# The convolution's part of the output projection for six of nine row tiles, computed among the attention heads

## The chip, the cores and the metric

The program runs on one core of a Trainium2 chip. The metric is device microseconds (us) of one execution. Three executions of the kernel before took 1584.36, 1586.79 and 1588.87 us, a median of 1586.79 us.

The engines are TensorE (PE, with its weight loads as PEld), VectorE (DVE), ScalarE (ACT), GpSimd (POOL) and SyncE (SP), which here issues the DMAs. Each works through its own instructions strictly in the order in which they are laid down.

## The reference

One layer of a streaming encoder: 1024 prompt rows, 8 samples of 16 rows (nine tiles of 128 rows in all) and D = 1024. One input projection feeds two branches. The first is differential attention: the prompt's rows look at the prompt, each sample at its cache of 1024 keys. The second is a gated causal convolution, a LayerNorm and a swish. One output projection joins both.

```python
z = h @ w_in
...
o = (rmsnorm(o, g_sub) * (1.0 - lam_init)).reshape(B, T, ATTN_WIDTH)
a, gate = jnp.split(zu, 2, axis=-1)
c = a * jax.nn.sigmoid(gate)
...
cv = jax.nn.silu(layernorm(depthwise_causal_conv(c_hist, w_conv, b_conv), ln_g, ln_b))
x = x + jnp.concatenate([o, cv], axis=-1) @ w_out
x = x + cross_attend(rmsnorm(x, g_cross), mk, mv, w_mq, g_mq, w_mo)
```

`o` and `cv` are 512 columns each, so `@ w_out` is the sum of two products with 512 rows of `w_out` each; the lower half, `cv @ w_out[512:]`, is what is moved here. The memory's keys and values (`mem @ w_mk`, `mem @ w_mv`) and an MLP complete the layer.

## The kernel before

All is float32. A product is computed as three matmuls on split operands (`mm3`, lines 123 to 125: high by high, high by low, low by high). A 128x512 block of the output projection from four blocks of 128 rows of `w_out` thus takes 12 matmuls of 512 columns.

The stages are: input projection and convolution taps (to about 297 us), attention (297 to 585 us), output projection (540 to 667 us), cross-attention, MLP. The taps leave the convolution's sums in DRAM (`dacc`).

The attention is written as generators that `weave` (L920) merges by position: each has a start and an end between 0 and 1 (`WP`, `WS`, `WL`, `WM`), and the one that is furthest behind is asked next. A scheduler then orders the instructions of each engine, with the offsets `PRI` as priorities. The generators:

- `prompt_stream` (L719): 4 heads of 8 tiles. A tile's scores go to a PSUM bank `sc` (2 banks), DVE adds the bias and finds the minimum (L679), ACT takes the exponential (L681), DVE joins the two maps (L688), PE transposes the weights (`pT`, bank `tr`, L699) and multiplies by the values (`po`, L704); the result goes to DRAM (`mix`).
- `sample_stream` (L834): per sample four loads of keys (`kr`, 512 KB, pool `wsk` of 4 buffers), transposes (`kT`), scores (`ss`), transposes of the weights (`wt`), four loads of values (`vu`), products (`spo`).
- `conv_norm` (L573): for each group of three tiles a load (`al`), transposes (`cvt`, bank `tr`), statistics and normalization on DVE (L584, L592), transposes back (`cvT`, L598), tanh and scale on ACT (L602, L604), two POOL operations (L605, L606), one store to DRAM (`dcv`, L607). It does so for four column tiles per group, with one buffer each of `sl` and `zt`.
- `memory_stream` (L856): two loads of memory tokens into buffers of the keys' pool, then the products `mk` and `mv` in the banks `sc`, with weights loaded as they come (`wmk`, `wmv`). Its operand is the tile `mem`, the only one of its pool.

After them `mixed_conv` (L1003) reads `dcv` back and splits it (L1008, L1009), and `proj_add` (L1047) multiplies: `n` is the half of the output columns, and tile `pj` the bank. The residual `x` is read from the input into `xr` (`load_xr`, L1043) and added by DVE (L1051). Then `mixed_attention` (L1011) reads `mix` back, transposes it (`omT`) and splits it, and `proj_add` multiplies by the upper half of `w_out`. The matmuls that read tile `MT` are the convolution's part, those that read `HC` the attention's.

Of the kernel before, what the change touches and what calls it, by code (L numbers as in the profile page):

```python
# [10 lines left out]
F32 = mybir.dt.float32  # L11
# [7 lines left out]
P = 128  # L19
# [34 lines left out]
TRS = ("tr", "sc", "tr", "sc", "kT", "sx")  # L54
WP, WS, WL, WM = (0, 1), (0, 1), (.2, .8), (.2, .8)
AB = {"rq": 2, "kS": 2, "rv": 4, "qs": 2, "p": (3, 1), "wT": 2}
# [3 lines left out]
def f32(ap):  # L60
    return ap.bitcast(F32)
# [3 lines left out]
def kernel(  # L65
# [53 lines left out]
    def load_w_plain(src, n, name, ring=None):  # L119
        return load_w([(lambda u: u[:, :n], src)], n, name, ring)  # L120
# [445 lines left out]
    dm = dram.tile([8, 8, 16, P], F32, name="dm")  # L566
    dcv = dram.tile([3, P, 4, 384], F32, name="dcv")
    PB = dict(PB1)
# [3 lines left out]

    def conv_norm():  # L573

        for g in range(3):
            xn = []
# [18 lines left out]
            for ct in range(4):  # L595
                ps = bk("tr", f"cvT{g}_{ct}")
                for j in range(3):
                    pe.transpose(ps[:, j * P:(j + 1) * P], xn[j][:, ct * P:(ct + 1) * P], ident)  # L598
                sg = wl.tile([P, 384], F32, name=f"sl{g}_{ct}", tag="sl", bufs=1)

                hg, hb = hln[:, ct:ct + 1], hln[:, 4 + ct:5 + ct]
                act.activation(sg, ps[:, :384], AF.Tanh, scale=hg, bias=hb)  # L602
                zt = wl.tile([P, 384], F32, name=f"zt{g}_{ct}", tag="zt", bufs=1)
                act.activation(zt, ps[:, :384], AF.Identity, scale=hg, bias=hb)  # L604
                pool.tensor_mul(sg, sg, zt)  # L605
                pool.tensor_add(zt, zt, sg)  # L606
                sp.dma_start(dcv[g, :, ct], zt)  # L607
                yield
# [243 lines left out]
    def mhalf(name):  # L852
        return rpool.tile([P, 512], F32, name=name, tag="r")


    def memory_stream():  # L856
        vm = []
        mh = wlm.tile([P, 2, 2, 4, 256], R32, name="mem", bufs=1)
        for t in range(2):
# [60 lines left out]
    def weave(*streams):  # L920

        live = [[it, n, a, z, 0, p] for it, n, a, z, p in streams]
        while live:
# [14 lines left out]
    wk = p2.enter_context(tc.tile_pool(name="wkA", bufs=2, reuse_waits="tile"))  # L938
    weave((prompt_stream(), 200, *WP, PRI[0]), (conv_norm(), 21, *WL, PRI[1]), (samples, 132, *WS, PRI[2]),
          (memory_stream(), 26, *WM, PRI[3]))  # L940
    p2.close()
# [61 lines left out]
    def mixed_conv(g):  # L1003
        mT[g][1] = new_group("m", g, 1)
        for c in range(4):
            zc = rpool.tile([P, 512], F32, name=f"zc{g}_{c}", tag="r")[:, :384]
            sp.dma_start(zc, dcv[g, :, c])
            act.copy(mT[g][1][:, 0, c, :], zc)  # L1008
            (pool if c % 2 else dve).tensor_sub(mT[g][1][:, 1, c, :], zc, f32(mT[g][1][:, 0, c, :]))  # L1009
# [33 lines left out]
    def load_xr(t):  # L1043
        for n in range(2):
            sp.dma_start(xr[t][n], xf[t][:, n * 512:(n + 1) * 512])

# [21 lines left out]

    def load_wo(k0, n):
        return [load_w_plain(w_out[0, (k0 + k) * P:(k0 + k + 1) * P, n * 512:(n + 1) * 512], 512, f"wo{n}_{k0 + k}")  # L1070
                for k in range(4)]

    for n in range(2):
        wo = load_wo(4, n)
        for g in range(3):
            if n == 0:
                mixed_conv(g)
            for t in range(3 * g, 3 * g + 3):
                if n == 0:
                    load_xr(t)  # L1080
                proj_add(mT, wo, t, n, 4)
    wo = load_wo(0, 0)
    for g in range(3):
        mixed_attention(g)
        for t in range(3 * g, 3 * g + 3):
            proj_add(mT, wo, t, 0)
    wo = load_wo(0, 1)
    memory_operands()
# [573 lines left out]
```

## Time and profile before

| | |
|---|---|
| three runs, median | 1586.79 us |
| profiled execution | 1584.48 us |
| its span, first to last instruction | 1582.7 us |
| mean granted clock of TensorE, share of full speed | 0.986 |
| PE busy | 1503.6 us, 95% |
| PEld busy | 1297.8 us, 82% |
| DVE busy | 1098.6 us, 69% |
| ACT busy | 733.0 us, 46% |
| POOL busy | 295.9 us, 19% |

The span is 1.8 us shorter than the execution. PE counts as busy from the start of a matmul to its modelled end; consecutive matmuls overlap, so a busy PE can still be waiting for operands between starts. Idle time in a view is that of an engine between its instructions, with what ended it.

### The profile page before, as it was taken

What the parts mean: (1) busy time and instruction counts of PE and PEld (TensorE: products, weight loads), DVE (VectorE), ACT (ScalarE), POOL (GpSimd) and SP (SyncE); (2) the same over time, 40 slices, a digit from 0 to 9 for tenths busy, and PEclk for the clock granted to TensorE, in tenths of its full rate; (3) what the DMA queues carried; (4) which work ended last, traced back from release to release, by engine and by line L of the source; (5) the groups of instructions that cost most, each with busy time, mean ns of one, the idle gap of its engine ahead of it and who ended that gap; (6) DMA issues with size and microseconds to landing.
All of it is one profiled execution on the core that took longest, in us unless ns stands there. A gap on an engine that the chain in (4) does not pass through costs nothing.

```text
span 1582.7 us, 25633 instructions
## 1 busy us (share of the span) xinstructions
PE 1503.6 (95%) x9326; PEld 1297.8 (82%) x9326; DVE 1098.6 (69%) x1984; ACT 733.0 (46%) x1530; POOL 295.9 (19%) x410
## 2 busy tenths in 40 slices
PE   7999989879899899999999899999999999999998
PEld 7989787667678688886679899999998887788887
DVE  5999999975756754535758776667565457995564
ACT  6312011486778642635656444444354443354442
POOL 5344682032544330231010000000000000000000
PEclk9999999999999999999999899999999999899999
DMA  6423242567776553103422654444384465653442
GB/s 196 145 82 100 84 136 98 187 210 233 234 243 213 194 168 106 51 24 114 145 85 88 191 179 132 160 156 151 125 259 156 142 206 184 218 172 94 124 135 93
DMA packets 187122, 237.88 MB, mean 150 GB/s; under 512 B 23851, under 2 KB 101717, under 8 KB 186996
## 3 DMA queue, kind: packets, MB, share of 16 engines
q1 hardware_dynamic: 186996, 236.25, 46.5%
q8 instruction: 73, 1.20, 0.3%
q14 instruction: 53, 0.43, 0.1%
HBM read 172.59 MB, written 63.60 MB: 149 GB/s over the span
## 4 chain that ended last, share of the span: by engine, by line
PE 67%; DVE 7%; ACT 5%; DMA 4%; issue 2%; POOL 1%; SPq 1%; DVEq 0%; ACTq 0%; POOLq 0%
PE p L123 13%; PE p L124 13%; PE p L125 13%; PE pj L123 3%; PE pj L125 3%; PE pj L124 3%; DVE acc L307 1%; PE po L704 1%; PE kT L768 1%; PE q L123 1%; PE q L124 1%; PE q L125 1%; PE z L124 1%; PE z L125 1%; PE z L123 1%
## 5 line engine op out<-in xcount | busy, mean ns | idle before, releaser
L124 PE MATMUL p<-Bp,Ap 128*128 128x512 f32 x448 | 176.6, 394 | 0.3 <-DVE Bp L1532 0.2
L125 PE MATMUL p<-Bp,Ap 128*128 128x512 f32 x448 | 176.1, 393 | 0.0
L307 DVE SCALAR_TENSOR_TENSOR acc<-cp,wc,acc 128x1024 f32<-128x1024 f32 (+2 forms) x150 | 167.5, 1119 | 1.2
L123 PE MATMUL p<-Bp,Ap 128*128 128x512 f32 x448 | 159.9, 393 | 7.0 <-ACT Bp L1531 6.0
L1531 ACT CAST Ap<-w_xb 128x512 fp32r<-128x512 f32 x112 | 69.5, 621 | 175.2 <-PE p L125 128.8
L1532 DVE TENSOR_TENSOR Ap<-w_xb,Ap 128x512 fp32r<-128x512 f32 x112 | 77.3, 690 | 102.7 <-ACT Ap L1531 102.6
L123 PE MATMUL p<-b_t,s 128*128 128x288 f32 x384 | 114.9, 299 | 6.2 <-ACT s L1284 6.2
L124 PE MATMUL p<-b_t,s 128*128 128x288 f32 x384 | 114.9, 299 | 0.0
L125 PE MATMUL p<-b_t,s 128*128 128x288 f32 x384 | 114.5, 299 | 0.0
L123 PEld LDWEIGHTS p<-Bp,Ap 128*128 128x128 f32 x448 | 84.2, 189 | 26.0 <-ACT Bp L1531 7.4
L124 PEld LDWEIGHTS p<-Bp,Ap 128*128 128x128 f32 x448 | 85.2, 190 | 19.4 <-DVE Bp L1532 1.4
L125 PEld LDWEIGHTS p<-Bp,Ap 128*128 128x128 f32 x448 | 85.2, 190 | 17.7
L124 PE MATMUL z<-wqkv,h 128*128 128x512 f32 x216 | 85.6, 396 | 1.7 <-DVE wqkv L116 1.6
L123 PE MATMUL z<-wqkv,h 128*128 128x512 f32 x216 | 86.2, 399 | 0.0
L125 PE MATMUL z<-wqkv,h 128*128 128x512 f32 x216 | 85.3, 395 | 0.0
L1368 ACT ACTIVATE o<-o 128x576 f32<-128x576 f32 x64 | 43.9, 686 | 79.9 <-DVE o L1378 32.3
L123 PEld LDWEIGHTS p<-b_t,s 128*128 128x128 f32 x384 | 73.4, 191 | 6.4 <-ACT s L1284 6.4
L123 PE MATMUL p<-b_b,a 128*128 128x288 f32 x256 | 75.8, 296 | 0.0
L124 PE MATMUL p<-b_b,a 128*128 128x288 f32 x256 | 75.7, 296 | 0.0
L125 PE MATMUL p<-b_b,a 128*128 128x288 f32 x256 | 75.6, 296 | 0.0
L124 PEld LDWEIGHTS p<-b_t,s 128*128 128x128 f32 x384 | 73.5, 191 | 0.0
L1051 DVE TENSOR_TENSOR XP<-pj,XP 128x512 f32<-128x512 f32 x54 | 37.1, 689 | 52.3 <-PE pj L125 52.1
(513 smaller groups left out, 4319.7 us busy)
## 6 DMA issues: line engine op xcount, KB each, us to landing
kr<-in_cache_k_dram SPq DMA_DIRECT2D x32, 512.0 KB
vu<-in_cache_v_dram SPq DMA_DIRECT2D x32, 512.0 KB
w1t<-in_w_ff_dram SPq DMA_DIRECT2D x32, 512.0 KB
w_xb<-ds SPq DMA_DIRECT2D x64, 256.0 KB
da<-o SPq DMA_DIRECT2D x48, 256.0 KB
w_xb<-da SPq DMA_DIRECT2D x48, 256.0 KB
ds<-o SPq DMA_DIRECT2D x32, 256.0 KB
dxr<-XP SPq DMA_DIRECT2D x18, 256.0 KB
```

The source lines that it names most:

```text
L123: pe.matmul(out, lh, rh, start=first, stop=False)
L124: pe.matmul(out, lh, rl, start=False, stop=False)
L125: pe.matmul(out, ll, rh, start=False, stop=last)
L307: dve.scalar_tensor_tensor(out=out, in0=cp[:, lo + j:hi + j], scalar=wj, in1=out, op0=ALU.mult, op1=ALU.add)
L704: pe.matmul(po, wT[:, j * P:(j + 1) * P], vss[h][jb][:, j], start=4 * jb + j == 0, stop=4 * jb + j == i)
L768: pe.transpose(ps[:, h * 256 + t * P:h * 256 + (t + 1) * P], kr[:, t, (2 * hp + h) * P:(2 * hp + h + 1) * P], ident)
L1051: dve.tensor_add(xr[t][n], ps, xr[t][n])
L1368: act.activation(c, c, AF.Relu)
L1531: act.copy(u[:, 0], src)
L1532: dve.tensor_sub(u[:, 1], src, f32(u[:, 0]))
```

## The change

Tiles 0 to 5 of the convolution's projection move into the attention. A new generator `conv_stream` is chained behind `memory_stream` as one stream of 68 steps: it loads the eight blocks of the lower half of `w_out`, runs `conv_norm` for groups 0 and 1, keeps the result in SBUF (`mc`, split at once, instead of by way of `dcv`), and for each of 6 tiles and 2 halves loads a half row block of `x` (`xc`), multiplies in a bank `sc` (tile `pc`), adds, and stores the sum to DRAM (`dxc`). Both `mc` and the memory's operand use the one buffer of tag `mem`. `load_xr` later reads `dxc` in place of the input. Group 2 (tiles 6 to 8) keeps the old way. `WL` becomes (.02, .3) and `WM` (.02, 1).

```diff
-WP, WS, WL, WM = (0, 1), (0, 1), (.2, .8), (.2, .8)
+WP, WS, WL, WM = (0, 1), (0, 1), (.02, .3), (.02, 1)
...
-    dcv = dram.tile([3, P, 4, 384], F32, name="dcv")
+    dcv = dram.tile([P, 4, 384], F32, name="dcv")
+    dxc = [dram.tile([P, D], F32, name=f"dxc{t}") for t in range(6)]
+    wo = [[], []]
...
-    def conv_norm():
-        for g in range(3):
+    def conv_norm(g, out):
+        if True:
...
-                sp.dma_start(dcv[g, :, ct], zt)
+                out(ct, zt)
                 yield
...
+    def conv_stream():
+        for n in range(2):
+            for k in range(4):
+                wo[n].append(load_wo(4, n, k))
+                if k % 2:
+                    yield
+        for g in range(2):
+            mc = wlm.tile([P, 4096], R32, name=f"mc{g}", tag="mem")[:, :3072].rearrange("p (h k c) -> p h k c", h=2, k=4)
+            def take(ct, zt):
+                act.copy(mc[:, 0, ct], zt)
+                dve.tensor_sub(mc[:, 1, ct], zt, f32(mc[:, 0, ct]))
+            yield from conv_norm(g, take)
+            for j in range(3):
+                t, c = 3 * g + j, slice(j * P, (j + 1) * P)
+                for n in range(2):
+                    xt = rpool.tile([P, 512], F32, name=f"xc{t}_{n}", tag="r")
+                    sp.dma_start(xt, xf[t][:, n * 512:(n + 1) * 512])
+                    ps = bk("sc", f"pc{t}_{n}")
+                    for k in range(4):
+                        mm3(ps, mc[:, 0, k, c], mc[:, 1, k, c], wo[n][k][:, 0], wo[n][k][:, 1], k == 0, k == 3)
+                        if k == 1:
+                            yield
+                    dve.tensor_add(xt, ps, xt)
+                    sp.dma_start(dxc[t][:, n * 512:(n + 1) * 512], xt)
+                    yield
...
-        mh = wlm.tile([P, 2, 2, 4, 256], R32, name="mem", bufs=1)
+        mh = wlm.tile([P, 4096], R32, name="mem", tag="mem").rearrange("p (a b c d) -> p a b c d", a=2, b=2, c=4)
...
-    weave((prompt_stream(), 200, *WP, PRI[0]), (conv_norm(), 21, *WL, PRI[1]), (samples, 132, *WS, PRI[2]),
-          (memory_stream(), 26, *WM, PRI[3]))
+    weave((prompt_stream(), 200, *WP, PRI[0]), (samples, 132, *WS, PRI[2]),
+          (conv_norm(2, lambda ct, zt: sp.dma_start(dcv[:, ct], zt)), 7, *WL, PRI[1]),
+          (chain(memory_stream(), conv_stream()), 68, *WM, PRI[3]))
...
-            sp.dma_start(xr[t][n], xf[t][:, n * 512:(n + 1) * 512])
+            sp.dma_start(xr[t][n], (xf[t] if t > 5 else dxc[t])[:, n * 512:(n + 1) * 512])
...
+    mixed_conv(2)
+    for t in (6, 7, 8, 0, 1, 2, 3, 4, 5):
+        load_xr(t)
     for n in range(2):
-        wo = load_wo(4, n)
...
+        for t in range(6, 9):
+            proj_add(mT, wo[n], t, n, 4)
```

Three places in PE's order show what moves. The first is at the first samples. Before, PE transposes the memory tokens (`memT`) beside the weights of the second sample (`wt1`), when it is at the prompt's tile 7 of head 0 (`sc0_7`); `kT2_` are the keys of the third sample:

```order
L674 MATMUL sc0_7_1_0_3451<-kS0_0_2759,qs0_1_3005 128x512
L675 MATMUL sc0_7_1_0_3451<-kS0_0_2759,ql1_2750 128x512
L768 MATMUL kT2_0_0_0_3557<-ident_69,kr2_0_3554 128x128 x2
L865 MATMUL memT0_0_3372<-ident_69,mem0_3370 128x128
L794 MATMUL ss1_2_3407<-k8_917,zq_915 32x128 x4
L865 MATMUL memT0_0_3372<-ident_69,mem0_3370 128x128 x3
```

After, they stand beside the weights of the first sample (`wt0`) and the keys of the second (`kr1_`), when the prompt is at tile 3 (`sc0_3` a few rows earlier) and its first product (`po0_0`) still stands behind them:

```order
L900 MATMUL memT0_1_2862<-ident_69,mem0_2847 128x128 x4
L771 MATMUL kT1_0_1_1_3400<-ident_69,kr1_1_3368 128x128 x4
L813 MATMUL wt0_8_3199<-ident_69,sp0_2733 128x128
L780 MATMUL ss1_0_3260<-ku1_0_1_3370,zq_915 32x256 x4
L771 MATMUL kT1_1_0_0_3445<-ident_69,kr1_2_3442 128x128 x4
L828 MATMUL spo0_3330<-vu0_0_3331,wt0_3123 32x128 x8
L828 MATMUL spo0_3330<-vu0_2_3430,wt0_3123 32x128 x8
L702 MATMUL pT0_0_0_2891<-ident_69,p0_0_0_2794 128x128
L771 MATMUL kT1_1_0_1_3480<-ident_69,kr1_2_3442 128x128 x4
L900 MATMUL memT1_0_2910<-ident_69,mem1_2908 128x128 x4
L707 MATMUL po0_0_2890<-vr0_0_2758,wT0_0_0_2893 128x128
```

The memory's work moved ahead by one sample, and the prompt's behind it.

The second place is the start of the second group's products, on PE, in the prompt's last head (`3_`): `pc3_0` and `pc3_1` are the two halves of tile 3, `wo0_5` is block 5 of the first half, `cvT1_3` the last column tile of the branch.

```order
L601 MATMUL cvT1_3_6057<-ident_69,xn5_5841 128x128
L123 MATMUL pc3_1_6195<-wo1_4_4538,mc1_5697 128x512
L124 MATMUL pc3_1_6195<-wo1_4_4538,mc1_5697 128x512
L125 MATMUL pc3_1_6195<-wo1_4_4538,mc1_5697 128x512
L123 MATMUL pc3_0_6112<-wo0_5_4449,mc1_5697 128x512
L124 MATMUL pc3_0_6112<-wo0_5_4449,mc1_5697 128x512
L123 MATMUL pc3_1_6195<-wo1_5_4543,mc1_5697 128x512
L124 MATMUL pc3_1_6195<-wo1_5_4543,mc1_5697 128x512
L125 MATMUL pc3_0_6112<-wo0_5_4449,mc1_5697 128x512
L125 MATMUL pc3_1_6195<-wo1_5_4543,mc1_5697 128x512
L707 MATMUL po3_0_6036<-vr3_0_5725,wT3_0_0_6039 128x128
```

The two halves run side by side, block by block; the next scores, `sc3_3_1`, stand behind the last block of both. Before, nothing like it stands there: the last head ran beside matmuls `pj` of tiles whose operands were complete, as here, with the prompt's tiles 4 to 6:

```order
L124 MATMUL pj3_0_6667<-wo0_5_6570,MT0_6552 128x512
L704 MATMUL po3_4_6223<-vr3_0_5568,wT3_4_0_6229 128x128 x4
L704 MATMUL po3_4_6223<-vr3_1_6037,wT3_4_1_6283 128x128
L674 MATMUL sc3_6_0_1_6323<-kS3_1_6044,qs3_1_6079 128x384
L675 MATMUL sc3_6_0_1_6323<-kS3_1_6044,ql1_2750 128x384
L674 MATMUL sc3_6_1_0_6347<-kS3_0_5575,qs3_1_6079 128x512
L675 MATMUL sc3_6_1_0_6347<-kS3_0_5575,ql1_2750 128x512
L125 MATMUL pj3_0_6667<-wo0_5_6570,MT1_6553 128x512
```

The scores moved behind the blocks of the branch. The third place is the end of the attention, on PE. Before, 26 matmuls `pj` stand between the last product `po3_7` and the first transpose `omT` of the attention's output, and 60 more among the transposes. After, two:

```order
L123 MATMUL pj8_1_6929<-wo1_7_4602,MT0_6812 128x512
L707 MATMUL po3_7_6754<-vr3_0_5725,wT3_7_0_6760 128x128 x4
L707 MATMUL po3_7_6754<-vr3_1_6221,wT3_7_1_6771 128x128 x4
L124 MATMUL pj8_1_6929<-wo1_7_4602,MT0_6812 128x512
L125 MATMUL pj8_1_6929<-wo1_7_4602,MT1_6813 128x512
L1073 MATMUL omT0_0_6969<-ident_69,om0_6963 128x128
```

The matmuls that stood behind the attention moved ahead of its end.

## Rows read from the trace of the kernel before

**Rows 1.** The page, part 1: span; busy us, share of the span, instructions of each engine.
```profile
span 1582.7 us, 25633 instructions
...
PE 1503.6 (95%) x9326; PEld 1297.8 (82%) x9326; DVE 1098.6 (69%) x1984; ACT 733.0 (46%) x1530; POOL 295.9 (19%) x410
```

**Rows 2.** Stretches of the attention: length, busy us (instructions) by engine, clock, DMA, GB/s.
```profile
297.00:380.00 83.00, 64.94 (x603) 47.81 (x603) 59.89 (x155) 62.40 (x150) 18.70 (x40) 0.94 0.70 230
380.00:500.00 120.00, 111.19 (x1130) 90.48 (x1132) 82.27 (x222) 93.37 (x218) 58.80 (x95) 1.00 0.75 235
500.00:540.00 40.00, 34.66 (x354) 28.57 (x353) 24.42 (x61) 31.14 (x77) 16.14 (x25) 0.91 0.52 169
540.00:608.00 68.00, 68.00 (x357) 57.14 (x358) 40.57 (x81) 26.91 (x62) 18.59 (x26) 1.00 0.55 181
```

**Rows 3.** The same view, the attention before the projection joins, as one stretch.
```profile
297.00:540.00 243.00, 210.79 (x2079) 166.85 (x2079) 166.58 (x436) 186.91 (x443) 93.64 (x159) 0.96 0.70 222
```

**Rows 4.** Timeline of PE: start us, us, instruction; two matmuls of the projection, twelve apart.
```profile
605.78 0.40 PE L124 MATMUL pj<-wo,MT 128*128 128x512 f32 x1
...
608.58 0.39 PE L124 MATMUL pj<-wo,HC 128*128 128x512 f32 x1
```

**Rows 5.** Chain of waits, all the program: start us, us, what; three loads on it.
```profile
340.33 4.31 DMA wmk_1r<-in_w_mk_dram
...
477.52 8.00 DMA wmv_3r<-in_w_mv_dram
...
533.46 4.69 DMA vu<-in_cache_v_dram
```

**Rows 6.** Chain of waits, 297 to 400 us; its short pieces of PE work.
```profile
338.98 0.23 PE sc L674
...
363.11 0.89 PE po L704 x8
364.00 0.45 PE kT L768 x4
```

**Rows 7.** The same view as rows 2, the stretch of the memory weights.
```profile
357.00:362.00 5.00, 4.96 (x48) 3.02 (x48) 2.01 (x5) 1.87 (x6) 1.95 (x2) 0.50 0.02 7
```

**Rows 8.** Tile view of the memory tokens, their loads: ns min/median/max, first and last start.
```profile
L861 SPq DMA_DIRECT2D mem<-in_mem_prompt_dram x2: 345/346/346, 319.1 to 326.7; - x2
```

**Rows 9.** Groups on DVE by form, 297 to 586 us: busy us, mean ns, idle before.
```profile
L641 DVE SCALAR_TENSOR_TENSOR ql<-qst,gqk,qs 64x512 fp32r<-64x512 f32 x16 | 12.0, 749 | 14.6 <-ACT qs L640 14.6
L629 DVE TENSOR_TENSOR kS<-kst,kS 64x512 fp32r<-64x512 f32 x16 | 11.0, 689 | 17.2 <-ACT kS L628 16.8
L679 DVE CUSTOM_DVE_ANT_0 p<-sc,biasm 128x512 f32<-128x512 f32 x16 | 11.0, 689 | 7.4 <-PE sc L675 6.9
...
L592 DVE TENSOR_SCALAR xn<-cvt,bmv,vrs 128x512 f32<-128x512 f32 x9 | 7.3, 806 | 1.0 <-POOL vrs L139 0.9
L584 DVE BATCH_NORM_STATS2 bst<-cvt 128x6 f32<-128x512 f32 x9 | 6.3, 695 | 0.5 <-PE cvt L582 0.4
...
L688 DVE SCALAR_TENSOR_TENSOR p<-p,cc,p 128x1024 f32<-128x1024 f32 x4 | 5.6, 1407 | 0.1
```

**Rows 10.** Tile views of the convolution branch: sl and zt, then zc.
```profile
L602 ACT ACTIVATE sl<-cvT,hln x12: 654/671/677, 388.1 to 516.8; 128x384 f32<-128x384 f32 x12
...
L605 POOL TENSOR_TENSOR sl<-sl,zt x12: 993/1008/1022, 389.4 to 518.5; 128x384 f32<-128x384 f32 x12
L606 POOL TENSOR_TENSOR zt<-zt,sl x12: 992/1004/1859, 390.5 to 519.6; 128x384 f32<-128x384 f32 x12
...
L1008 ACT CAST MT<-zc x12: 499/513/518, 539.4 to 560.3; 128x384 fp32r<-128x384 f32 x12
L1009 DVE TENSOR_TENSOR MT<-zc,MT x6: 554/686/1105, 540.4 to 559.9; 128x384 fp32r<-128x384 f32 x6
```

**Rows 11.** Tile views of the projection and of the attention products: first and last start.
```profile
L123 PE MATMUL pj<-wo,HC x72: 390/394/484, 608.3 to 666.1; 128*128 128x512 f32 x72
...
L704 PE MATMUL po<-vr,wT x288: 270/275/422, 314.8 to 584.7; 128*128 128x128 f32 x144
```

More of the change, by code (lines that the diff above doesn't have):

```diff
@@ L853, in mhalf, with load_wo @@
         return rpool.tile([P, 512], F32, name=name, tag="r")
+    def load_wo(k0, n, k):
+        return load_w_plain(w_out[0, (k0 + k) * P:(k0 + k + 1) * P, n * 512:(n + 1) * 512], 512, f"wo{n}_{k0 + k}")
+    def conv_stream():
[23 more added lines that the diff above has]
+                    yield
     def memory_stream():
         vm = []
-        mh = wlm.tile([P, 2, 2, 4, 256], R32, name="mem", bufs=1)
+        mh = wlm.tile([P, 4096], R32, name="mem", tag="mem").rearrange("p (a b c d) -> p a b c d", a=2, b=2, c=4)
         for t in range(2):
@@ L1006, in mixed_conv @@
             zc = rpool.tile([P, 512], F32, name=f"zc{g}_{c}", tag="r")[:, :384]
-            sp.dma_start(zc, dcv[g, :, c])
+            sp.dma_start(zc, dcv[:, c])
             act.copy(mT[g][1][:, 0, c, :], zc)
@@ L1067, in square_sum @@
         return ms2
-    def load_wo(k0, n):
-        return [load_w_plain(w_out[0, (k0 + k) * P:(k0 + k + 1) * P, n * 512:(n + 1) * 512], 512, f"wo{n}_{k0 + k}")
-                for k in range(4)]
+    mixed_conv(2)
+    for t in (6, 7, 8, 0, 1, 2, 3, 4, 5):
+        load_xr(t)
     for n in range(2):
-        wo = load_wo(4, n)
[L1075 to L1082, printed above, removed]
+        for t in range(6, 9):
+            proj_add(mT, wo[n], t, n, 4)
+    wo = [load_wo(0, 0, k) for k in range(4)]
     for g in range(3):
@@ L1086 @@
             proj_add(mT, wo, t, 0)
-    wo = load_wo(0, 1)
+    wo = [load_wo(0, 1, k) for k in range(4)]
     memory_operands()
```

## The prediction

> **What bounds the kernel now.** I read the page's first part, then the attention by stretches, then the chain of waits, then the groups and tiles of the steps that move. PE is busy 95% of the span, more than any other engine [rows 1]. The change takes no matmul away: it moves 6 tiles x 2 halves x 12 = 144 matmuls of 512 columns. Two of the projection start 2.80 us apart with twelve between them, so one costs 0.233 us [rows 4] and the 144 cost 33.5 us, before and after. Its whole effect is thus on PE's waits.
>
> Where are they? In 297 to 540 us PE is busy 210.8 of 243 us: 32.2 us idle, 18.1 of them in the first 83 us, 8.8 in the next 120, 5.3 in the next 40 [rows 2, 3]. From 540 to 608 us, where the conv products now stand among the last head, it is never idle and the clock is full [rows 2]. So the products are already a filler: they hide the waits of the last head, and the change takes 144 of 216 away from there and puts them where idle time is left. The question is whether they fill it, and what they uncover.
>
> The upper bound of a gain is the 32.2 us. A busy share counts overlapped matmuls as busy, so the weight loads are a second reading: they fill 57.1 of the 68 us of the packed stretch, 0.840, and 166.9 of the 243 us, 0.687 [rows 2, 3]. At the packed rate the 243 us hold 166.9 / 0.840 = 198.6 us of work, which leaves 44.4 us of waits. The Trainium skill (Perfetto Trace Analysis, Identifying the Most-Contended Engine) also holds that matmul busy time is a bad measure and that the weight loads' share is the better one; by it the room is 44 us instead of 32. The two shares here differ in that sense; which one the chip pays back no row shows, so it is one of the rivals below.
>
> **The change, part by part.**
>
> *Early, 297 to about 375 us.* WM starts at .02 instead of .2. The memory tokens, loaded at 319 and 327 us before [rows 8], go into two of the four `kr` buffers of the first two samples instead of a later one. The keys' third and fourth loads of the second sample must then wait until the tokens are transposed, and a 512 KB load follows with about 4.7 us in the like of it on the chain [rows 5]; the order leaves about 1 us of PE work as cover for each. By the second sample's weights the order has done 16 instead of 48 `sc` matmuls, 6 instead of 21 `pT`, 3 instead of 21 `po` and 12 more transposes. With 0.23 us for `sc`, 0.45 for four transposes and 0.89 for eight `po` [rows 6] that is 7.4 + 1.7 + 2.0 - 1.3 = 10 us of prompt work less to hide behind. By the third sample 48 earlier `mk` matmuls of 256 columns (half of 0.233 each, 5.6 us) and the prompt's catching up make most of it good. What can go away is a stall on `wmk` (4.31 us on the chain [rows 5]) and its sequel: from 357 to 362 us PE ran at 0.50 of its clock (the lower level, 1.2 GHz) for 5 us, 2.5 us lost, after it had stood with little to do [rows 7]. Two loads uncovered, 7 us, less that stall, 4 to 5 us: I take +2. Bounds: -13 (most of the 18.1 us idle filled) to +10 (all lost cover uncovered).
>
> *Middle, 380 to 540 us.* The 72 products of group 0 (16.8 us) stand among samples whose PE idles 8.8 + 5.3 = 14.1 us [rows 2]. Their operands are complete when they begin. Part of this idle is a wait for a load that comes whatever PE does: `wmv` 8.0 us, `vu` 4.7 us on the chain [rows 5]. I take half, -7. Bounds: -14 to 0.
>
> *The late hole, at the third head's end.* `mc` has one buffer, so group 1's branch may write its operand only when the 72 products of group 0 are through; the order puts its `cvt` transposes right behind `pc2_1`, where the last head also begins. From there to the first column tile DVE stands in order before four reductions (0.689), three statistics (0.695), three normalizations (0.806), two pairs for the next head (0.689 and 0.749) and a joining of the two maps (1.407) [rows 9]: 2.8 + 2.1 + 2.4 + 2.9 + 1.4 = 11.6 us, with the short operations between about 18 us (an estimate: half of it again). PE has about 11 us of work there by the rows of the order (scores, transposes and products at the times above). Then `pc3_0` and `pc3_1` take both `sc` banks, and each of their blocks waits for a column tile: tanh and scale on ACT (0.671 and, of the same form, again 0.671), two on POOL (1.008, 1.004), the copy (0.513) and the difference on DVE (0.554 to 0.686), 4.5 us [rows 10], one after the other, since `sl` and `zt` have one buffer. Three behind the first are 13.5 us, against about 10 us of PE work: 24 products at 0.233, 5.6 us, and transposes, `po` and scores for 4.5 more. The next scores, `sc3_3_1`, stand behind the last block, so ACT and DVE get nothing new from the prompt and it is not caught up. Holes of 7 + 3.5: I take +10. Bounds: +3 (only the column tiles) to +16 (no cover in either, and a lower clock behind them).
>
> *Banks and transfers.* Twelve times `pc` takes one of the two `sc` banks of the prompt or of `mk`/`mv`, and its addition on DVE must free it. Twelve loads `xc` and twelve stores `dxc` of 256 KB are 6.3 MB, less eight stores `dcv` of 197 KB: 4.7 MB more over about 200 us, 23 GB/s on 222 [rows 3], a DMA share of 0.77 instead of 0.70. There is room, but the samples' loads get later. `xc` is hidden by 12 products (2.8 us) only in part. No row shows a `pc`; nearest are the `sc` groups, whose DVE idle before is 7.4 us over 16 [rows 9], 0.46 each. I take +1. Bounds: 0 to 12 x 0.46 = +6.
>
> *The end of the attention.* Before, 86 `pj` stand around and behind the last `po` (584.7 us) before the attention's own start at 608.3 [rows 11]; they hide `mix` on its way through DRAM, the transposes and the split. After, two of the conv products are left and the 72 attention products of tiles 0 to 5 (16.8 us), whose operands were stored long before, cover the last group. The first transposes have less ahead of them. I take +1. Bounds: 0 to +9 (the 608.3 - 584.7 = 23.6 us less 14.6 of other work). The additions `xr` and the splits saved on POOL and DVE stand beside a busy PE and are worth nothing.
>
> Sum: 2 - 7 + 10 + 1 + 1 = +7 us. Against the profiled execution's 1584.5 us (the span of 1582.7 and 1.8 around it) that is 1591.5; the median of the three runs is 2.3 us above it, so I predict 1593.8, rounded 1594.
>
> **The rivals.** *Faster.* The products and the earlier memory work fill idle PE, and the hole stays short, because scores of the last head that stand ahead of the first block feed DVE. Place: 297 to 540 us. Price: early -6 (a third of the 18.1 us), middle -10, hole +4, the rest 0: -12, 1575 us. For it: 32 us idle, and an operand that is ready. Against: the order has both `sc` banks taken while column tiles are made. It decides when the hole is below some 6 us.
>
> *Much faster.* If the waits are the 44.4 us that the weight loads show and half are filled in all stretches, -22: 1565 us. Against it, the longest waits end on loads. The reading of the weight loads as the measure is the skill's page named above.
>
> *No change.* Filled idle and the new hole cancel: -7 to -9 against +7 to +9, 1587 us. This needs only that the early term is -3 instead of +2 and the hole 8.
>
> *Not done as said.* In the order all 144 products stand ahead of the last `po`; this rival is out.
>
> **How the numbers follow.** What a measurement of this kernel can't tell from no change is 0.3%, 4.8 us. The forecast, slower, has 0.44, with its own range +2 to +18; some of it lies inside the 4.8 us, as some of the other cases does, and I let these cancel. No change 0.24, faster 0.26, much faster 0.06; both faster cases are 0.32. The range: below 1573 lies the much faster case and a little of the faster, about 0.1; above 1607 (+20, hole and early term both at their upper ends) another 0.1.
>
> **What would show it.** In the trace after: PE idle and a wait for ACT or DVE at the products of tile 3 (hole of 10 us; under 6 the rival is right); PE idle in the stretch of the second sample's keys no less than before, ending on a `kr` load; idle in 380 to 500 us near 4 instead of 8.8; a short idle between the last `po` and the attention's products. The last `po` should come some 26 us later than 584.7 (before, 130 of the 216 products stood ahead of it, now 214: 84 x 0.233 = 19.6 us, and the 6 us of the terms ahead of it), and the last product of the projection some 7 us later. It is wrong if the products of tile 3 start without a wait, if the early idle of 18 us shrinks by more than half, or if loads in the middle come so late that idle grows there.

## The result: slower by 26 us, where 7 were forecast

The changed kernel took 1612.5 us (median of 4 runs, 1608.2 to 1616.2), the kernel before beside it 1586.0: a ratio of 1.0167, interval [1.0144, 1.0190]. The direction was forecast, the size was not: +7 was predicted, and the time lies above the range. The profiled execution took 1608.2 us; its span against that of before [rows 1]:

```profile
span 1606.5 us, 25648 instructions
...
PE 1512.4 (94%) x9326; PEld 1302.0 (81%) x9326; DVE 1096.2 (68%) x1984; ACT 733.8 (46%) x1530; POOL 291.9 (18%) x410
```

1606.5 against 1582.7: 23.8 us, with the same 9326 matmuls on PE. Its busy time is 8.8 us longer, so a part of the loss lies inside what counts as busy. The same stretches as in [rows 2], with the last head divided where its events divide it (length, then busy us of PE, PEld, DVE, ACT, POOL, clock, DMA share, GB/s):

```profile
297.00:380.00 83.00, 67.78 (x615) 51.60 (x616) 52.10 (x137) 56.76 (x135) 28.53 (x47) 0.88 0.74 245
380.00:500.00 120.00, 106.37 (x1079) 87.00 (x1077) 70.76 (x185) 88.65 (x207) 50.11 (x75) 0.99 0.73 237
500.00:533.00 33.00, 33.00 (x318) 26.16 (x320) 21.75 (x59) 18.42 (x45) 4.48 (x12) 1.00 0.55 178
533.00:558.00 25.00, 15.62 (x94) 12.58 (x84) 15.84 (x41) 12.20 (x28) 6.65 (x13) 0.80 0.22 69
558.00:578.00 20.00, 14.84 (x70) 10.80 (x70) 9.37 (x21) 13.35 (x34) 9.49 (x16) 0.91 0.04 11
578.00:626.00 48.00, 46.60 (x243) 37.48 (x243) 27.86 (x67) 18.85 (x46) 8.91 (x17) 1.00 0.63 211
```

The samples end at 533 us instead of 539. From there to the last `po` the kernel before took 46 us with PE never idle; now it takes 92, and PE is idle 9.4 of the first 25 us and 5.2 of the next 20, with a clock of 0.80 and 0.91. The last `po` starts at 625.5 us (584.7 before [rows 11]; forecast some 26 us later, it came 41 later):

```profile
L707 PE MATMUL po<-vr,wT x288: 270/275/582, 330.7 to 625.5; 128*128 128x128 f32 x144
```

A busy PE can still be waiting, so I made a finer account, an estimate from the traces: the spacing of starts where matmuls follow one another closely (0.232 us for 512 columns and in proportion, 0.109 a transpose, 0.111 a `po` matmul, 0.057 one of 32 rows) is PE's work between two events; what is left is waits, a lower clock among them. By this account, in us:

| | before | after | difference | predicted |
|---|---|---|---|---|
| 297 us to the third sample's weights | 24.4 | 22.5 | -1.9 | +2 |
| from there to the last sample product | 17.6 | 13.2 | -4.4 | -7 |
| from there to the last `po` (the last head) | 0.8 | 28.4 | +27.6 | +10, +1 |
| from there to the last transpose for the cross-attention | 1.2 | 4.0 | +2.8 | +1 |
| sum | 44.1 | 68.1 | +24.0 | +7 |

Each column rests on one execution. In the control (run 8 below), whose time is that of the kernel before, the same account gives some 2 us less up to the last sample product, so the other three lines are not far above the noise. Nearly the whole miss, 16.6 of 17 us, is in the third line. What PE does there, its timeline (start, length, instruction, idle before and its releaser):

```profile
536.70 0.40 PE L678 MATMUL sc<-kS,ql 128*128 128x512 f32 x1
538.72 0.63 PE L585 MATMUL cvt<-ident,al 128*128 128x128 f32 x4 [1.62 <-DVE xn L595]
541.11 0.63 PE L622 MATMUL qst<-ident,r 128*128 128x128 f32 x4 [1.77 <-DVE kS L632]
543.20 0.48 PE L677 MATMUL sc<-kS,qs 128*128 128x128 f32 x1 [1.46 <-ACT qs L643]
...
552.65 0.70 PE L702 MATMUL pT<-ident,p 128*128 128x128 f32 x4 [1.39 <-DVE xn L595]
...
557.89 0.50 PE L123 MATMUL pc<-wo,mc 128*128 128x512 f32 x1 [0.75 <-ACT mc L872]
...
573.21 0.51 PE L123 MATMUL pc<-wo,mc 128*128 128x512 f32 x1 [2.56 <-ACT mc L872]
```

The transposes of the second group's branch (`cvt`, `cvT`) and those of the last head (`kst`, `qst`) wait in turn for DVE and ACT, and PE has nothing else to do. DVE, in the same stretch, works off both chains in order, statistics, keys, statistics, the joining of two maps:

```profile
534.57 0.69 DVE L587 BATCH_NORM_STATS2 bst<-cvt 128x6 f32<-128x512 f32 x1
...
538.64 0.68 DVE L632 TENSOR_TENSOR kS<-kst,kS 64x512 fp32r<-64x512 f32 x1
...
539.44 0.68 DVE L587 BATCH_NORM_STATS2 bst<-cvt 128x6 f32<-128x512 f32 x1
...
541.09 1.25 DVE L691 SCALAR_TENSOR_TENSOR p<-p,cc,p 128x1024 f32<-128x1024 f32 x1
```

Then the products wait for the column tiles. The tanh of the four, on ACT:

```profile
553.91 0.67 ACT L605 ACTIVATE sl<-cvT,hln 128x384 f32<-128x384 f32 x1
...
557.75 0.67 ACT L605 ACTIVATE sl<-cvT,hln 128x384 f32<-128x384 f32 x1
...
563.51 0.67 ACT L605 ACTIVATE sl<-cvT,hln 128x384 f32<-128x384 f32 x1
...
567.95 0.67 ACT L605 ACTIVATE sl<-cvT,hln 128x384 f32<-128x384 f32 x1
```

They start 14.0 us apart from first to last, 13.5 were forecast. What PE waited for in the last head, by line waited for (total us, times, longest):

```profile
PE pc L123 <- ACT mc L872: 3.6, 3, 2.6
PE sc L677 <- ACT qs L643: 2.4, 2, 1.5
PE pT L702 <- DVE xn L595: 1.8, 2, 1.4
PE qst L622 <- DVE kS L632: 1.8, 1, 1.8
```

No single wait is large: head, branch and products wait for each other, with no other matmul ready. Where were the 72 products left for tiles 6 to 8? Their operand `MT` is written only behind the last moved product:

```profile
L125 PE MATMUL pc<-wo,mc x48: 392/396/775, 483.3 to 600.6; 128*128 128x512 f32 x48
```

```profile
L1044 ACT CAST MT<-zc x4: 509/511/513, 601.0 to 609.1; 128x384 fp32r<-128x384 f32 x4
```

The last `pc` starts at 600.6, the first cast into `MT` at 601.0 (539.4 before [rows 10]): `MT` lies in the memory of `mc`, as run 5 confirms.

### The profile page after: what moved, and what is told of

The parts are those of the page before. It is cut to its first block, busy times and chain, and to the rows that moved or that the text cites. A ratio compares the mean times of both kernels' runs of the same rounds, so it can differ in the third digit from the quotient of the medians.

```text
span 1606.5 us, 25648 instructions
## 1 busy us (share of the span) xinstructions
PE 1512.4 (94%) x9326; PEld 1302.0 (81%) x9326; DVE 1096.2 (68%) x1984; ACT 733.8 (46%) x1530; POOL 291.9 (18%) x410
## 4 chain that ended last, share of the span: by engine, by line
PE 75%; DVE 10%; DMA 6%; ACT 4%; issue 2%; POOL 1%; SPq 1%; ACTq 0%; DVEq 0%; POOLq 0%
PE p L123 12%; PE p L124 12%; PE p L125 12%; PE z L124 3%; PE z L125 3%; PE z L123 3%; PE pj L123 3%; PE pj L124 2%; PE pj L125 2%; DVE acc L307 2%; PE po L707 2%; DVE acs L328 1%; PE kT L771 1%; PE q L124 1%; PE q L123 1%
## 5 line engine op out<-in xcount | busy, mean ns | idle before, releaser
L125 PEld LDWEIGHTS p<-Bp,Ap 128*128 128x128 f32 x448 | 84.7, 189 | 17.6
L123 PEld LDWEIGHTS p<-b_t,s 128*128 128x128 f32 x384 | 73.1, 190 | 7.2 <-ACT s L1313 7.1
L124 PEld LDWEIGHTS p<-b_t,s 128*128 128x128 f32 x384 | 73.2, 191 | 0.0
L125 PEld LDWEIGHTS p<-b_t,s 128*128 128x128 f32 x384 | 72.6, 189 | 0.0
```

What stands on the lines that cost most here:

```text
L123: pe.matmul(out, lh, rh, start=first, stop=False)
L124: pe.matmul(out, lh, rl, start=False, stop=False)
L125: pe.matmul(out, ll, rh, start=False, stop=last)
```

## The experiments

A difference is that of medians, the kernel before beside each. "Head" is the third line of the table, the waits from the last sample product to the last `po` (after: 28.4, before: 0.8). In the expectations, theory A is that the branch among the last head is the loss, B that the head alone is, C the locked memory, D the later start of the head, E the missing cover.

**1. The branch by way of DRAM.** The second group's branch early, woven from .02 to .3 with the third group's; its result goes to DRAM and is read back where the branch stood.

```diff
-            yield from conv_norm(g, take)
+            if g == 0:
+                yield from conv_norm(g, take)
+            else:
+                for ct in range(4):
+                    ...
+                    sp.dma_start(zc, dcv[0, :, ct])
+                    take(ct, zc)
```

> After with the second group's branch (normalization, tanh, products with the gate) taken out of the last head: it runs early, as it did before the change, stores to DRAM, and the operand of tiles 3 to 5 is read back and split (one copy, one difference a column tile) where the branch stood. Theory A (the branch makes the hole: its operations stand in order on DVE, ACT and POOL, and the products wait for column tiles while they hold both score banks): the 28 us of PE waits from the last sample product to the last attention product fall to some 10, time 1592 to 1598. Theory B (the last head begins alone, its own chain of transposes, queries and small scores leaves PE without ready work, and the branch is innocent): over 20 us of waits stay, time 1606 or more.

Measured: 1598.8 us, ratio 1.0085 [1.0067, 1.0103], 13.7 us below the changed kernel; head 14.0. Theory A holds for half of the loss, a little outside its range. The other 12 us are not the branch's operations; the products still wait for an operand, now for the read back and split one: the second group's first product starts at 549.5 us, 12.4 behind the last sample product. Its windows at the head's start:

```profile
537.00:560.00 23.00, 18.71 (x116) 15.52 (x108) 15.93 (x44) 13.15 (x37) 2.58 (x8) 0.93 0.37 117
560.00:580.00 20.00, 17.36 (x96) 13.72 (x95) 14.05 (x35) 12.34 (x32) 4.96 (x13) 1.00 0.27 86
```

Some idle time stays at the head's start, but far less than in 533 to 578 us of the changed kernel, where PE was busy 30.5 of 45 us.

**2. Three tiles.** Only the first group's 72 products are moved (`for g in range(1)`).

> After with only the first group (tiles 0 to 2, 72 products) moved into the attention; tiles 3 to 8 are done as before the change, so 144 products are again ready for the last head. If the second group is the whole loss: the waits of the last head go back to some 1 us, the 6 us gained up to the last sample product stay, and the time is 1578 to 1584, below the kernel before. If moving the cover away costs in proportion to the products moved: half of the loss stays, 1598.

Measured: 1597.3 us, 1.0070 [1.0054, 1.0086]; head 12.5. The time is that of the second expectation. The second group is not the whole loss: 72 products moved alone cost 10.6 us. They stand at 517 to 572 us, in the last head, and the projection of tiles 3 to 8, the cover that should have stayed, starts only behind them, at 573.4 us (539.9 before).

**3. The memory early, no product moved.** In the kernel before, `WM` = (.02, .395).

> The kernel before with one edit: the memory's stream is woven from .02 to .395 of the attention (as it stands in the changed kernel) instead of .2 to .8; no product is moved. If the 6 us gained up to the last sample product in the changed kernel come from the earlier memory work: 1580 to 1583. If they come from the first group's products beside the samples: no gain or a loss, 1586 to 1590 (the prediction's early term was +2).

Measured: 1586.6, 0.9997 [0.9986, 1.0009]. No effect: the 6 us gained up to the last sample product are not the memory's. As far as this edit shows, the early term of the prediction should have been 0.

**4. The second group's products in the bank `ss`.**

```diff
-                    ps = bk("sc", f"pc{t}_{n}")
+                    ps = bk("ss" if g else "sc", f"pc{t}_{n}")
```

> After with the second group's products in the bank of the samples' scores (one bank, idle once the samples are through) instead of the two banks of the prompt's scores; the branch stays where it is. Theory A holds two parts: if the score banks held by the products of tile 3 are the larger part, 8 us or more go, time 1604 or less; if the order on DVE and ACT is, under 3 us go, 1610 to 1613. Theory B: no change, 1612.

Measured: 1625.2, 1.0243 [1.0229, 1.0256]. Inconclusive for its question: the last sample's scores need the same bank, and in this run they came behind the products (its last product at 615 us, behind the last `po`). Sharing a bank with a stream that isn't through moves that stream.

**5. to 8. Another place in SBUF.** `mc` no longer lies under `MT`, in the changed kernel (run 5), with three tiles (6), in run 1's kernel (7) and in the kernel before (8):

```diff
-    wlm = p2.enter_context(tc.tile_pool(name="wkM", ...))
     ws = p2.enter_context(tc.tile_pool(name="wkS", ...))
+    wlm = p2.enter_context(tc.tile_pool(name="wkM", ...))
...
-    xr = [[xps[1 - h // 9][...
+    xr = [[xps[h // 9][...
```

> After with only the places in SBUF exchanged: the pool of the products' operand (mc) is laid down after the samples' pool instead of before it, and the two halves of the residual trade places. mc then lies under the residual of tiles 0 to 4, which is read after the products anyway, and no longer under the projection's operand MT of tiles 6 to 8. Theory C (the projection's remaining products are ready but locked out, because their operand lies in the memory of mc, which the last moved product reads): the projection's products start before the last pc, and of the 28 us of waits from the last sample product to the last attention product 5 to 8 go, since only 72 products are left and the order lets them in at tiles 4 and 5; time 1604 to 1608. Theory A (the branch alone): no change, 1612.

Measured in run 5: 1614.0, 1.0179 [1.0152, 1.0206]; head 28.0. The lock is real, and it is gone:

```profile
L1044 ACT CAST MT<-zc x4: 513/514/515, 589.1 to 597.0; 128x384 fp32r<-128x384 f32 x4
```

The first cast comes at 589.1 instead of 601.0, before the last `pc` (607.7 here). But nothing is won: at that point the long waits are over. My expectation, 5 to 8 us of waits less, failed.

> Three tiles moved (72 products), with the exchanged places. Three tiles alone took 1597.3 us, with 12.5 us of waits in the last head and its first product of the projection right after the last pc. Theory C: 144 products are ready for the last head as before the change, its waits fall from 12.5 to some 3, time 1586 to 1589. Theory D (the loss is the memory's and the products' displacement of the prompt, which comes later against the samples, and no cover helps): 1596 or more.

Measured in run 6: 1592.0, 1.0038 [1.0024, 1.0052]; head 7.8, the projection's first product at 548.1 instead of 573.4. With 144 products to let in, the open lock gives back 5.2 of the 10.6 us; 8 to 11 were expected.

> Six tiles, the second group's branch early and by way of DRAM, with the exchanged places (without: 1598.8 us, 14.0 us of waits in the last head and 5.9 behind it). Theory C: 6 to 9 of the 20 us go, time 1590 to 1593; with theory A alone nothing is left to win here, 1598.

Measured in run 7: 1606.0, 1.0117 [1.0096, 1.0138], head 17.3. 7 us worse than without the exchange (the intervals just overlap); the expectation failed, and I did not find out why.

> The kernel before with nothing but the exchanged places, as a control for the runs beside it. All theories: no difference beyond 0.2%, 1584 to 1590, since the memory's operand there is read for the last time at 509 us, before the samples end and before the projection can start.

Measured in run 8: 1585.8, 0.9999 [0.9985, 1.0012]. The control holds.

**9. No cover.** In the kernel before, all 216 conv products behind the attention's first half of the projection.

```diff
-    for n in range(2):
-        wo = load_wo(4, n)
-        ...
     wo = load_wo(0, 0)
     for g in range(3):
         mixed_attention(g)
         ...
+    for n in range(2):
+        wo = load_wo(4, n)
+        ...
```

> The kernel before with all 216 conv products put behind the attention's first half of the projection; the order then has none of them ahead of the last attention product, and head and samples stand as before. It measures what the last head waits when nothing covers it. Theory E (the last head needs the cover, whoever takes it away pays): from the last sample product to the last attention product 15 to 25 us of waits, against 0.8, time 1601 to 1610. Theory D (a last head that starts beside the samples, as here at 504 us, needs little cover; in the changed kernel it starts 31 us later, behind the samples, and that is the loss): under 10 us of waits, time 1588 to 1596.

Measured: 1602.0, 1.0094 [1.0074, 1.0114]: 15.2 us slower. Head 10.4, and 7.6 (1.2 before) from the last `po` on. The time is that of theory E; the head's own waits lie between the two theories, 9.6 more than before, and 6.4 more come behind the head. The first 26 us of the bare head:

```profile
540.00:566.00 26.00, 20.63 (x138) 16.18 (x127) 16.37 (x44) 13.05 (x34) 5.88 (x12) 0.93 0.74 248
```

That is the price of the cover in the kernel before, some 10 us of it in the head. The prediction had described this cover and not put it into its sum.

**10. The prompt ahead.** After, with `WP` = (0, .9).

> After with the prompt's stream woven from 0 to .9 instead of 0 to 1, nothing else. The last head then starts in the order about 7 us of PE work earlier, though by then the samples too are nearly through. Theory D: the waits of the last head (28 us) fall by a third or more, time 1598 to 1604. Theory A (the branch among the last head) and theory E: more of the branch and of the products falls behind the head, so less cover: 1608 to 1618.

Measured: 1609.5, 1.0136 [1.0115, 1.0157]; head 23.8, but 9.4 behind it. 3 us less than the changed kernel, with intervals that overlap: not a gain clear of noise, and not what theory D asked.

**11. The stream to .85.** After, with `WM` = (.02, .85).

> After with the memory's and the conv stream woven to .85 instead of to 1: the second group's branch and 16 more of its products stand among the samples, the last head starts still later in the order. Theory A (the branch among the last head): waits there fall from 28 to about 14, as with the branch by way of DRAM, time 1597 to 1601. Theory D: the head starts later and is alone longer, no gain: 1610 to 1616.

Measured: 1602.8, 1.0096 [1.0075, 1.0117], 9.7 us below the changed kernel. Head 22.7, and only 31.1 up to the last sample product (after: 35.7, before: 42.0). Between the expectations: the branch beside the samples is cheaper, and more of the samples' waits is filled, yet the last head keeps most of its waits. Its last ready product stands at 590.9 us, and 10.8 of the 22.7 us come in the 24.4 us from there to the last `po`; the other 12 stand beside products and are not explained. Theory D had expected no gain.

**12. Three tiles, places exchanged, the prompt to .9.**

> Three tiles moved, the places exchanged, and the prompt woven to .9 (without it: 1592.0 us, 7.8 us of waits in the last head). Theory D: the head starts as early against the samples as in the kernel before, its waits go to 2 or 3 us and the 4 us gained up to the samples' end stay, time 1582 to 1587. Theory E: 24 products instead of 95 cover the head, its waits grow to 15, time 1598.

Measured: 1605.0, 1.0108 [1.0086, 1.0129]; head 11.3 and 7.4 behind it. Theory D falls. With 24 instead of 95 products of the projection ahead of the last `po`, the same three tiles take 13 us more, 7 above theory E's figure. By the traces only 3.5 of the added waits are in the head and 6.4 behind it; some 6 come ahead of the last sample product, which starts at 537.9 instead of 526.9 us, and are not the cover's.

**13. The branch late, cover kept.** The kernel before with `WL` = (.45, 1).

> The kernel before with one edit: the convolution's branch is woven from .45 to 1 instead of from .2 to .8, so that the third group's branch (tiles 6 to 8) stands among the last head, where 144 products of the other two groups remain as cover; no product is moved. If the branch costs by itself (its operations stand in order on DVE, ACT and POOL ahead of the head's): 10 us or more over the kernel before, 1596 or more. If it costs only where the cover is gone: within 4 us of it, 1583 to 1591.

Measured: 1589.8, 1.0025 [1.0010, 1.0040]; head 6.5: 5.7 more waits there, of which 4.5 are gained back ahead of it. Only the second half of the branch came to lie in the head: its last normalization ends at 528.9 us, before the last sample product (532.4), and its column tiles follow from 535 to 564. Those cost 2 us on balance where 144 ready products stand beside them; the statistics were not tried there:

```profile
532.00:578.00 46.00, 42.84 (x250) 35.72 (x242) 27.97 (x62) 26.16 (x58) 20.56 (x27) 0.96 0.55 183
```

**14. The second branch left out.** Tiles 3 to 5 use the first group's operand.

> After with the second group's branch left out (tiles 3 to 5 are multiplied with the first group's operand); all 144 products moved as in the change. If branch and cover add up: the branch's 14 us go and no more, 1597 to 1600, as with the branch by way of DRAM. If the products waiting for it are all of the loss: 1588 or less.

Measured: 1586.9, 0.9996 [0.9982, 1.0010]; head 11.0. All of the loss in time is gone, 25.6 us by the medians. By the traces it is 20 of the 23.8 us: 17.4 of the head's waits and the 24 transposes left out (24 x 0.109 = 2.6). The time is that of the second expectation, but not for its reason: run 17 gives the products' own wait a small part. Branch and cover do not add up, as the first expectation had it. With no branch in between, the 72 products of tiles 3 to 5 start 3.4 us behind the last sample product (526.6 against 523.2) and are the cover of the head, which begins behind the samples here as well:

```profile
523.00:540.00 17.00, 15.82 (x96) 13.26 (x87) 11.19 (x25) 9.28 (x19) 1.20 (x4) 0.90 0.33 102
540.00:560.00 20.00, 19.56 (x115) 16.04 (x114) 12.47 (x36) 9.73 (x32) 4.62 (x11) 1.00 0.32 103
```

**15. and 16. Three tiles, earlier.** `WM` to .85 and to .7, places exchanged.

> Three tiles moved, places exchanged, the memory's and the conv stream woven to .85 instead of 1; all 144 products left are ahead of the last attention product in the order. Theory E (cover for the last head, and products only where the samples wait): with the 5 us or more gained up to the samples' end and 3 us or less of waits in the head, 1580 to 1586. If three moved tiles still cost: 1592, as with the stream to 1.

> The same with the stream woven to .7, so that the 72 products stand all ahead of the last head. If the samples' waits are what the products fill, more of them is filled: 1579 to 1585. If the products then only push the prompt back: 1590 or more.

Measured: 1610.2, 1.0152 [1.0136, 1.0168], and 1596.4, 1.0068 [1.0045, 1.0091]. Run 15 missed both of its cases; run 16 came out as its second, 1590 or more. Run 15 has 51.6 us of waits up to the last sample product instead of 38.0 with the stream to 1, which is not explained here, and 12.9 in the head with all 144 products there. In run 16 the samples' waits are filled as with six tiles (6.3 us less than before), but the prompt is pushed back: its last `po` starts at 611.5 us (584.7 before), and the cover is used up too soon. Its 144 products end at 583.3. The head up to there and from there on:

```profile
532.00:584.00 52.00, 50.63 (x286) 42.39 (x279) 34.37 (x79) 28.34 (x68) 13.19 (x22) 1.00 0.47 159
584.00:611.00 27.00, 20.79 (x122) 16.08 (x122) 18.62 (x50) 15.05 (x37) 6.88 (x15) 0.95 0.22 61
```

Of its 14.0 us of waits in the head 11.4 fall into the bare end. In run 15, where the products end at 609.8 and the last `po` starts at 626.6, it is 6.2 of 12.9. It is thus not enough that products are ready when the head begins: they must last to its end.

**17. The branch not awaited.** The second branch in its place, stored to DRAM and not used; tiles 3 to 5 read the first group's operand.

> After with the second group's branch done in its place, but its result stored to DRAM and not used: the products of tiles 3 to 5 read the first group's operand and wait for nothing. If the products' wait for the column tiles (with both score banks held) is the loss: 1590 or less. If it is the branch's own operations among the last head's: 1605 or more. The prediction gave the first part of the hole 7 us and the waiting products 3.5, which would put it near 1604.

Measured: 1607.4, 1.0121 [1.0089, 1.0153]: 5 us below the changed kernel, though the intervals overlap; head 25.2, 3.2 less. It is the second expectation. In its order the branch and the head stand alone behind the samples (last sample product at 535.7 us); the products, though they wait for nothing, stand behind and start at 556.2:

```profile
533.00:549.00 16.00, 9.82 (x75) 7.46 (x73) 12.61 (x28) 7.68 (x15) 2.97 (x6) 0.87 0.41 123
549.00:558.00 9.00, 6.79 (x29) 5.87 (x29) 4.58 (x16) 4.56 (x15) 1.97 (x6) 0.69 0.03 8
```

PE is busy 16.6 of 25 us, at 0.87 and 0.69 of the clock; with the branch left out (run 14) it is busy 35.4 of 37. So the wait of the products with their two banks is the small part, 3 to 5 us, and most of the loss comes from the stretch ahead of them.

No version beats the kernel before; the nearest that computes the whole layer with products moved is run 6, three tiles with the places exchanged, 0.38% slower.

## Why the prediction was right in sign and wrong in size

**What bounds it.** Right: PE's work is the same, PE's waits are all that moves (+24.0 of waits, +23.8 of span).

**Early.** Predicted +2, measured -1.9, which is not clear of noise; run 3 gives 0 for the memory's move alone. Two uncovered loads did not show as such: no wait for a load is in PE's list from 297 to 380 us. It waits there for the copies of the keys on ACT (`ku`), 10.4 us instead of 5.7, and less for the rest.

**Middle.** Predicted -7, measured -4.4. The sign holds, and the gain is there in runs 11 and 14 too and not in run 3; in run 1 it lies ahead of the third sample's weights instead. I had taken half off for loads that come whatever PE does; in PE's own waits before, from 380 to 540 us, only 1.8 us end on a load (`vu`). The mark that I named failed by the plain windows: idle time from 380 to 500 us did not fall to 4, it is 13.6 against 8.8, where the first group's products start only at 482.4; 500 to 533 us has none. That the misses of these two terms, -3.9 and +2.6, nearly cancel is luck.

**The late hole: the step that failed.** The prediction's sentence was "Holes of 7 + 3.5: I take +10". The place and the kind of wait were right; the first hole was sized at less than half. It was 18 us of DVE's operations less "about 11 us of work" of PE. By the account above, 24.8 us pass from the last sample product (533.1) to the first product of tile 3 (557.9), with 9.4 of PE work in them: 15.4 us of waits instead of 7. PE's work is only 1.6 below the estimate; the length is 6.8 above it. The branch's first statistics start 1.5 us behind the last sample product. From there to the first tanh it is 19.3 us instead of 18. And 4.0 us are the first column tile's own way from its tanh (553.9) to the product: the prediction priced that way at 4.5 us for each of the three tiles behind the first, and left it out for the first. DVE, whose operations were to set the length, is itself busy only 15.8 of the 25 us from 533 to 558: head and branch hand every piece from PE to DVE or ACT and back, and both wait. The second hole, to the last column tile's product (573.2), has 15.3 us with 8.7 of work, 6.6 of waits instead of 3.5. The remaining 6.4 us come from there to the last `po`. In all of this a lower clock is included.

What stands behind the missing length is that nothing else was ready for PE, and this the sum had no term for. Its first part says that the 216 products "hide the waits of the last head" and that 144 are taken away, and the only terms at that end are banks and the tail, +1 each. Run 9 shows that cover to be worth 15.2 us, some 10 of them in the head. And what decides is not how many products the order puts there, but whether one is ready all through the head. In the changed kernel the branch stands between the two groups of products: the first 72 are used up at 531.7 us, the next 72 wait for the branch, and the last 72 stand behind them, locked out besides by the memory of `mc`. Run 14 (no branch, products ready at once) takes the loss away; run 13 (column tiles in the head, products beside them) has 2 us of it, run 1 (branch elsewhere, products still waiting for their operand) 12. In runs 9, 11 and 16 a head without branch, in a stretch without products, has 10.4, 10.8 and 11.4 us of waits. So the bare head alone waits some 11 us, and with the branch among it 28. With products beside it the head alone waited 0.8 us (before), the head with half of the branch 6.5 (run 13). Branch and cover are thus one cause, a stretch without a ready product, and not a sum of two, as far as half a branch can show it.

**Banks, transfers, the end.** +1 and +1 against 6.4 behind the hole (banks, clock and the rest not told apart) and +2.8. The DMA rate rose and no load became the wait of the last head.

**The rivals.** "Faster" named the right turning point, the hole, and the wrong side of it. "Much faster": by the weight loads, 297 to 533 us now hold 164.8 / 0.840 = 196.2 us of work in 236, 39.8 us of waits instead of 44.4, against 28.9 us of PE's idle time. The Trainium skill (Perfetto Trace Analysis, Identifying the Most-Contended Engine) calls the weight loads' share a better measure than matmul busy time. These traces agree in so far as the waits are more than the idle time: the finer account, which does not use the weight loads, finds 35.7 us in the same stretch. The changed kernel filled some 5 of the 44 us, not 22.

Open: how the branch's cost divides between its operations on DVE and its transposes on PE in the head's chain; what the 11 to 12 us of waits that runs 11 and 14 keep in the head beside ready products are; why the exchanged places harm the version by way of DRAM; why .85 is a bad position for three tiles.

## What to carry to other kernels

Before work is moved out of a packed stretch, price the stretch bare: what it hides is a term of the sum, and one run with the filler put behind shows it (here 15 us). In the new order, look for the stretch where no independent matmul is ready on any list, between the last product of one batch and the first operand of the next, or behind the last product of all, and count its whole length: every step of the chain, the first piece's own way included, and not the busy time of one engine. A branch that makes the next batch's operand is cheap where ready products stand beside it (2 us in run 13, for its second half). The memory that holds the operand should not lie under that of the work that could fill the gap; with three tiles moved this was worth 5.2 us, with six nothing.

## What the runs showed of the hardware

In the last head of the changed kernel TensorE's granted clock fell to its lower level (1.2 GHz) three times, each time behind waits of PE (in the 8 us from 533 to 541, at full clock, it was busy 4.7):

```profile
542.90:549.60 6.70, 5.07 (x21) 4.38 (x21) 2.90 (x6) 2.96 (x8) 1.05 (x4) 0.50 0.14 41
553.20:556.40 3.20, 2.70 (x13) 2.34 (x12) 0.87 (x3) 1.95 (x5) 1.10 (x2) 0.50 0.00 0
573.70:576.90 3.20, 3.20 (x12) 2.42 (x10) 1.08 (x3) 1.59 (x4) 0.00 (x0) 0.50 0.10 26
```

The 0.80 of 533 to 558 us and the 0.91 of the next 20 are means over both levels. With products beside the column tiles of the same kind of branch (run 13) the mean was 0.96. A hole thus costs its neighbours too: matmuls of the products that start 0.23 us apart at full clock start 0.40 to 0.43 us apart from 573.5 to 574.8 us, right behind a wait of 2.6 us. The three stretches hold some 5 us of PE's work at full clock, so at most as much of the head's 28.4 us is the clock (an estimate by the account above).
